# Smallest query tile of a sparse-attention stage: scores of two heads in one PSUM bank, maxima subtracted by VectorE, one exponential for four heads, and the units of the two small tiles alternated

## The chip, the cores and the metric

One core of one Trainium2 chip runs the kernel. The metric is the device time of one execution in microseconds (us); below, PE is TensorE, PEld its weight loads, DVE is VectorE, ACT is ScalarE, POOL is GpSimd and SP is the queue that issues most transfers.

## The reference, cut to what matters

A two-layer decoder trunk on 512 positions of width 1024. Layer 0 mixes with a gated linear recurrence and retention, layer 1 with sparse attention; each layer has a SwiGLU feed-forward part. The change lies in layer 1's attention. With 512 positions there are 8 blocks of 64, so the top 16 blocks are all blocks and the window of 512 covers everything: both the "selected" and the "window" branch are plain causal attention, each with its own keys and values.

```python
# 16 heads in 4 groups of 4; 64 elements a head; per branch: own k, v
s = jnp.einsum('bqgrd,bkgd->bgrqk', qb, kw)
p = jax.nn.softmax(jnp.where(causal, s, NEG), axis=-1)
o_branch = jnp.einsum('bgrqk,bkgd->bqgrd', p, vw)
o = gate0 * o_cmp + gate1 * o_slc + gate2 * o_win   # o_cmp: 31 compressed blocks
return o.reshape(B, QB, HD)                         # and then out @ w_out
```

## The kernel before, in words

All heavy products are done as three float32r products of a high and a low part (hi·hi, hi·lo, lo·hi). Before the attention stage the kernel runs layer 0 with its feed-forward part and layer 1's input projections; after it comes the output projection (`ps_p`, in `layer1`, with weights `w1o`), then the second feed-forward part.

`attention` cuts the 512 queries into four tiles of 128. Tile i sees (i+1)·128 keys. The order is tile 2, tile 3, tile 1, tile 0. The work is a list of units. For tiles 2 and 3 a unit is one group of 4 heads and one branch; for tiles 1 and 0 a unit is one group and both branches, so u.n is 2. That makes 8 + 8 + 4 + 4 = 24 units, numbered 0 to 23: units 16 to 19 are tile 1, units 20 to 23 are tile 0. The loop runs n from 0 to 26 in slots, at least four for each n. Three units are in work at once:

- unit n has its heads done, one head r in each slot. `head_s` (lines 1154 to 1167) puts the scores of one head for its branches in one PSUM bank (two products with the keys, hi and lo, and one product that adds the causal mask on the last 128 keys); `head_m` (L1171) takes the negated maximum on DVE; `head_e` (L1175) takes one exponential per branch on ACT, with the maximum as its bias; each is followed by a second instruction that reads out the row sum.
- unit n-1 is normalized: `norm` (L1179, L1180) takes reciprocals on DVE and multiplies them by the gates on POOL, `scale` (L1185) multiplies each head and branch on POOL.
- unit n-3 has its probability blocks of 128 keys turned and multiplied by the values, one block in each slot: `block_t` (L1190, four transposes on PE), `block_hi` (L1194, ACT), `block_lo` (L1197, DVE), `block_v` (L1205, L1206; at a group's end also L1211, L1212 for the compressed branch). `finish` (L1217 ACT, L1222 twice on DVE, L1226 ACT, L1228 POOL) then writes the group's output `o` as hi and lo parts, `oh` and `ol`.

Work of other kinds is given out a step at a time by `advance` from the list `side`: the steps of `finish`, the stacking of a tile's queries (`late`), and the compressed branch (`compressed`: scores on PE, mask and maximum on DVE, subtraction on POOL, exponential on ACT, sums on DVE, multiplication on POOL, transposes, hi and lo copies). The last product of a group (`br == 1 and j == u.i`) needs the tile's compressed probabilities:

```python
while u.i not in cmp_pt:
    advance()
```

The probabilities of a unit lie in a ring of four buffers (`probs`, tile `wr`), which is the ring that the weights are loaded to as well: the transfers of `w1o` wait for buffers of the last units. Scores have four PSUM banks (`psA`), transposes two (`psC`), outputs two (`psB`). A planner puts the instructions of each engine in order from the order of the program, shifted by the offsets of `high_priority`, and from its own estimates of when each is ready; on the chip every engine then runs its list strictly in that order.

Of the kernel before, what the change touches and what calls it, by code (L numbers as in the profile page):

```python
# [17 lines left out]
F32 = mybir.dt.float32  # L18
F32R = mybir.dt.float32r
AF = mybir.ActivationFunctionType  # L20
ALU = mybir.AluOpType
AX = mybir.AxisListType
PSUM = bass.MemoryType.PSUM

P = 128
# [8 lines left out]
G = 4  # L34
# [29 lines left out]
class Trunk:  # L64
# [1018 lines left out]
    def attention(self, QS, stack, stacked, qlate, halves, KH, KL, VV, kc2, vc, gate, OH, OL, fill):  # L1083
# [3 lines left out]
        V, A, Q, T = nc.vector, nc.scalar, nc.gpsimd, nc.tensor  # L1087
# [61 lines left out]
        def make(i, g, bs):  # L1149
            u = Unit()  # L1150
            u.i, u.g, u.bs, u.nk, u.n = i, g, bs, (i + 1) * P, len(bs)
            u.heads = [(u, r) for r in range(R)]
            u.blocks = [(u, b, j) for b in range(u.n) for j in range(i + 1)]
            return u

        def head_s(u, r):
            if r == 0:
                u.p = self.probs().rearrange("p (r b x) -> p r b x", r=R, b=u.n)
                u.rs = self.sm.tile([P, R, u.n], F32, tag="rs", name="rs")
                u.kh, u.kl = (x[u.g // 2][:, u.bs[0]:u.bs[-1] + 1, u.g % 2, 0:u.nk] for x in (KH, KL))  # L1160
            h = R * u.g + r
            ps = self.psA("ps_s")
            u.ps = ps[:, 0:u.n * u.nk].rearrange("p (b x) -> p b x", b=u.n)
            q = QS[u.i][:, h, :]
            T.matmul(u.ps, q, u.kh, start=True, stop=False)
            T.matmul(u.ps, q, u.kl, start=False, stop=False)
            T.matmul(u.ps[:, :, u.i * P:u.nk], self.identr, self.triNeg.unsqueeze(1).broadcast_to([P, u.n, P]), start=False, stop=True)

        def head_m(u, r):
            u.nm = self.sm.tile([P, 2], F32, tag="nm", name="nm")  # L1170
            V.tensor_reduce(u.nm[:, 0:u.n], u.ps, axis=AX.X, op=ALU.max, negate=True)  # L1171

        def head_e(u, r):
            for b in range(u.n):
                A.activation(u.p[:, r, b, 0:u.nk], u.ps[:, b, :], AF.Exp, bias=u.nm[:, b:b + 1], accum_out=u.rs[:, r, b:b + 1])  # L1175

        def norm(u):
            gb = gate[:, u.i, :].rearrange("p (h b) -> p h b", b=3)[:, R * u.g:R * u.g + R, u.bs[0] + 1:u.bs[-1] + 2]
            V.reciprocal(u.rs, u.rs)  # L1179
            Q.tensor_tensor(u.rs, u.rs, gb, op=ALU.mult)  # L1180

        def scale(u, r):
            for b in range(u.n):
                x = u.p[:, r, b, 0:u.nk]
                Q.tensor_tensor(x, x, u.rs[:, r, b:b + 1].broadcast_to([P, u.nk]), op=ALU.mult)  # L1185
# [43 lines left out]
            yield  # L1229

        tiles = halves[0] + halves[1]
        units = [make(i, g, bs) for i in tiles for g in range(G) for bs in (((0,), (1,)) if i >= 2 else ((0, 1),))]
        side = [compressed(tiles[0])]

        def advance():
# [7 lines left out]
        for n in range(len(units) + LAG):  # L1243
# [9 lines left out]
            for sl in range(max(R, nb)):  # L1253
# [5 lines left out]
                if hd:  # L1259
                    head_s(*hd)  # L1260
                if bl:
                    block_t(*bl)
                if hd:
                    with prio(offset=12):
                        head_m(*hd)
                if bl:
                    block_hi(*bl)
                if hd:
                    with prio(offset=-6):
                        head_e(*hd)  # L1270
# [3 lines left out]
                if un and sl < R:  # L1274
                    if sl == 0:
                        with prio(offset=-6):
                            norm(un)
                    scale(un, sl)
                if len(pend) >= 2:
                    args = pend.pop(0)  # L1280
                    block_v(*args)
                    u, b, j = args[:3]
# [145 lines left out]
```

## Time and profile before

| | |
|---|---|
| median of 3 runs | 1245.33 us (1245.04 to 1245.99) |
| the profiled execution, its own time | 1245.73 us |
| its span, first to last instruction | 1243.8 us |
| busy, whole span: PE, DVE, ACT, POOL | 98%, 64%, 55%, 19% |
| attention units 16 to 23, with what follows up to the gapless projection | 781.5 to 846.5 us |

The times of runs are made without the profiler's span: the profiled execution's own time is 1.9 us longer than its span, and 0.4 us longer than the median. Shares of busy time are averages over stages with different limits, so the stretch of the change is read by itself. [...]

### The profile page before, as it was taken

To read this page: it belongs to the slowest core of one execution; us is meant where nothing else is said; L and a number is where in the kernel's file an instruction comes from. 1 tells how busy PE (TensorE), PEld (TensorE's weight loads), DVE (VectorE), ACT (ScalarE), POOL (GpSimd) and SP (SyncE) were. 2 spreads that over 40 slices of the span, in tenths; PEclk is the share of its full clock that TensorE was granted. 3 is DMA by queue.
4 is the path that set the end of the run, shared out by engine and by line. 5 is a ranking of instruction groups with operands and counts; after the bars stand their busy time and mean duration, and the time that the engine had idled before them with its cause. 6 is when DMAs were issued, how large, how long until landed. Compare 5 with 4: busy or idle time off the path is not lost.

```text
span 1243.8 us, 16442 instructions
## 1 busy us (share of the span) xinstructions
PE 1221.5 (98%) x6077; PEld 1031.4 (83%) x6077; DVE 799.1 (64%) x1237; ACT 686.3 (55%) x1395; POOL 232.0 (19%) x303
## 2 busy tenths in 40 slices
PE   9999999999999999999999999999999999999997
PEld 7688888888888889988888878877888888888996
DVE  6886629666356636674364889986776537653764
ACT  6541447664256426655454688995666336633653
POOL 0001420220012002100000568680111011101200
PEclk9999999999999999999999999999999999999998
DMA  9122143784388328852100000134488358824832
GB/s 342 68 102 68 35 169 102 172 191 150 98 191 178 138 64 182 228 194 71 66 35 1 1 1 1 35 113 159 108 197 186 120 120 185 201 82 106 181 93 68
DMA packets 35535, 149.23 MB, mean 120 GB/s; under 512 B 3936, under 2 KB 6256, under 8 KB 26624
## 3 DMA queue, kind: packets, MB, share of 16 engines
q1 hardware_dynamic: 21296, 100.88, 22.8%
q0 software_dynamic: 14016, 47.27, 21.4%
q8 instruction: 48, 0.79, 0.2%
q14 instruction: 31, 0.25, 0.1%
q10 hardware_dynamic: 144, 0.04, 0.0%
HBM read 143.98 MB, written 4.19 MB: 119 GB/s over the span
## 4 chain that ended last, share of the span: by engine, by line
PE 88%; ACT 5%; DVE 4%; POOL 1%; issue 1%; DMA 0%; POOLq 0%; DVEq 0%; SPq 0%; ACTq 0%
PE ps L203 6%; PE ps L201 6%; PE ps L202 6%; PE ps_t L201 5%; PE ps_X L201 5%; PE ps_X L203 5%; PE ps_X L202 5%; PE ps_t L203 5%; PE ps_t L202 5%; PE ps_V L201 3%; PE ps_V L203 3%; PE ps_V L202 3%; ACT prob L1175 2%; PE ps_Y L201 2%; PE ps_Z L203 2%; PE ps_Z L201 2%
## 5 line engine op out<-in xcount | busy, mean ns | idle before, releaser
L136 ACT CAST whi<-wr 128x512 fp32r<-128x512 f32 (+1 forms) x540 | 295.1, 593 | 348.1 <-PE ps L202 126.2
L137 DVE TENSOR_TENSOR wlo<-wr,whi 128x1024 fp32r<-128x1024 f32 (+2 forms) x272 | 313.3, 1154 | 208.9 <-ACT whi L136 205.4
L201 PE MATMUL ps<-gh,whi 128*128 128x512 f32 (+1 forms) x364 | 139.8, 384 | 0.0
L203 PE MATMUL ps<-gh,wlo 128*128 128x512 f32 (+1 forms) x364 | 139.2, 382 | 0.0
L202 PE MATMUL ps<-gl,whi 128*128 128x512 f32 (+1 forms) x364 | 139.1, 382 | 0.0
L161 POOL DMA_DIRECT2D wr<-wff x64 | 55.6, 868 | 366.8 <-DVE wlo L137 327.8
L201 PE MATMUL ps_t<-whi,hgh 128*128 128x512 f32 x288 | 114.7, 399 | 0.0
L202 PE MATMUL ps_t<-wlo,hgh 128*128 128x512 f32 x288 | 113.3, 394 | 0.0
L203 PE MATMUL ps_t<-whi,hgl 128*128 128x512 f32 x288 | 112.7, 391 | 0.0
L201 PE MATMUL ps_X<-whi,sg 128*128 128x512 f32 (+1 forms) x288 | 107.2, 372 | 0.0
L203 PE MATMUL ps_X<-whi,sg 128*128 128x512 f32 (+1 forms) x288 | 106.9, 371 | 0.0
L202 PE MATMUL ps_X<-wlo,sg 128*128 128x512 f32 (+1 forms) x288 | 106.8, 371 | 0.0
L1185 POOL TENSOR_TENSOR prob<-prob,rs 128x384 f32<-128x384 f32 (+3 forms) x128 | 88.1, 722 | 1.9
L767 DVE TENSOR_TENSOR h<-ps,h 128x512 f32<-128x512 f32 x46 | 31.8, 691 | 82.6 <-PE ps L203 82.6
L203 PEld LDWEIGHTS ps<-gh,wlo 128*128 128x128 f32 x364 | 68.4, 188 | 13.3
L202 PEld LDWEIGHTS ps<-gl,whi 128*128 128x128 f32 x364 | 68.4, 188 | 13.2
L201 PEld LDWEIGHTS ps<-gh,whi 128*128 128x128 f32 x364 | 68.4, 188 | 13.0
L1175 ACT ACTIVATE prob<-ps_s,nm 128x384 f32<-128x384 f32 (+3 forms) x128 | 68.2, 540 | 15.8 <-DVE nm L1171 14.9
L201 PE MATMUL ps_V<-whi,sg 128*128 128x512 f32 (+1 forms) x192 | 71.2, 371 | 0.0
L202 PE MATMUL ps_V<-wlo,sg 128*128 128x512 f32 (+1 forms) x192 | 71.2, 371 | 0.0
L203 PE MATMUL ps_V<-whi,sg 128*128 128x512 f32 (+1 forms) x192 | 71.2, 371 | 0.0
L203 PEld LDWEIGHTS ps_t<-whi,hgl 128*128 128x128 f32 x288 | 54.1, 188 | 11.5 <-issue 0.2
(316 smaller groups left out, 2568.6 us busy)
## 6 DMA issues: line engine op xcount, KB each, us to landing
wr<-wff POOLq DMA_DIRECT2D x64, 512.0 KB, 5.9
wr<-wff SPq DMA_DIRECT2D x24, 1024.0 KB, 4.8
wr<-wfg POOLq DMA_DIRECT2D x32, 384.0 KB, 5.8
wr<-w0t SPq DMA_DIRECT2D x10, 1024.0 KB, 5.9
wr<-w1t SPq DMA_DIRECT2D x10, 1024.0 KB, 4.9
wr<-wfg SPq DMA_DIRECT2D x12, 768.0 KB, 4.3
wr<-w2a SPq DMA_DIRECT2D x8, 1024.0 KB, 4.8
wr<-w2c SPq DMA_DIRECT2D x8, 1024.0 KB, 5.0
```

Of the source, the lines that this page charges most:

```text
L136: self.nc.scalar.copy(hi[:, c], x[:, c])
L137: self.nc.vector.tensor_tensor(lo, x, hi.bitcast(F32), op=ALU.subtract)
L161: self.nc.gpsimd.dma_start(x[:, c], more[:, c], accum_op=ALU.add)
L201: mm(ps, ah, bh, start=(first and k == 0), stop=False)
L202: mm(ps, ah, bl, start=False, stop=False)
L203: mm(ps, al, bh, start=False, stop=(last and k == n - 1))
L767: V.tensor_tensor(hm, ps, hm, op=ALU.add)
L1175: A.activation(u.p[:, r, b, 0:u.nk], u.ps[:, b, :], AF.Exp, bias=u.nm[:, b:b + 1], accum_out=u.rs[:, r, b:b + 1])
L1185: Q.tensor_tensor(x, x, u.rs[:, r, b:b + 1].broadcast_to([P, u.nk]), op=ALU.mult)
```

## The change

For tile 0 alone (u.i == 0):

- `head_s` puts the scores of two heads, both branches, in one bank; the mask is added once for the pair, on 512 columns.
- `head_m` takes the maxima once for the pair (four maxima of 128 elements each, 512 in all), not negated.
- `head_e` subtracts the maxima on DVE, from PSUM into the probability buffer, once for each pair; after the fourth head ACT takes one exponential of the unit's 1024 elements in place, without bias and without row sums.
- `norm` takes the row sums on DVE, one reduction over 1024 elements.
- `scale` multiplies both branches of a head in one POOL instruction.

The list of units becomes tile 1, tile 0, tile 1, tile 0, and so on, a group at a time: units 16, 18, 20, 22 are tile 1 and units 17, 19, 21, 23 are tile 0.

```diff
         def head_s(u, r):
             ...
+            q = QS[u.i][:, h, :]
+            if u.i == 0:
+                if r % 2 == 0:
+                    u.ps = self.psA("ps_s").rearrange("p (r b x) -> p r b x", r=2, b=2)
+                T.matmul(u.ps[:, r % 2], q, u.kh, start=(r % 2 == 0), stop=False, skip_group_check=True)
+                T.matmul(u.ps[:, r % 2], q, u.kl, start=False, stop=False, skip_group_check=True)
+                if r % 2:
+                    T.matmul(u.ps.rearrange("p r b x -> p (r b) x"), self.identr, self.triNeg.unsqueeze(1).broadcast_to([P, 4, P]), start=False, stop=True, skip_group_check=True)
+                return
         ...
         def head_m(u, r):
-            u.nm = self.sm.tile([P, 2], F32, tag="nm", name="nm")
+            if u.i == 0 and r % 2 == 0:
+                return
+            u.nm = self.sm.tile([P, 4], F32, tag="nm", name="nm")
+            if u.i == 0:
+                V.tensor_reduce(u.nm, u.ps.rearrange("p r b x -> p (r b) x"), axis=AX.X, op=ALU.max)
+                return
             V.tensor_reduce(u.nm[:, 0:u.n], u.ps, axis=AX.X, op=ALU.max, negate=True)
         def head_e(u, r):
+            if u.i == 0:
+                if r % 2:
+                    x = u.p[:, r - 1:r + 1, :, 0:P].rearrange("p r b x -> p (r b) x")
+                    V.tensor_tensor(x, u.ps.rearrange("p r b x -> p (r b) x"), u.nm.unsqueeze(2).broadcast_to([P, 4, P]), op=ALU.subtract)
+                if r == 3:
+                    x = u.p[:, :, :, 0:P].rearrange("p r b x -> p (r b) x")
+                    A.activation(x, x, AF.Exp)
+                return
             ...
         def norm(u):
             ...
+            if u.i == 0:
+                V.tensor_reduce(u.rs.rearrange("p r b -> p (r b)"), u.p[:, :, :, 0:P].rearrange("p r b x -> p (r b) x"), axis=AX.X, op=ALU.add)
             V.reciprocal(u.rs, u.rs)
             ...
         def scale(u, r):
+            if u.i == 0:
+                x = u.p[:, r, :, 0:P]
+                Q.tensor_tensor(x, x, u.rs[:, r, :].unsqueeze(2).broadcast_to([P, 2, P]), op=ALU.mult)
+                return
             ...
-        units = [make(i, g, bs) for i in tiles for g in range(G) for bs in (((0,), (1,)) if i >= 2 else ((0, 1),))]
+        units = [make(i, g, bs) for i in halves[0] for g in range(G) for bs in ((0,), (1,))]
+        units += [make(i, g, (0, 1)) for g in range(G) for i in halves[1]]
```

## Rows read from the trace of the kernel before

**Rows 1.** The page, part 1: busy us, share of the span, instructions.
```profile
PE 1221.5 (98%) x6077; PEld 1031.4 (83%) x6077; DVE 799.1 (64%) x1237; ACT 686.3 (55%) x1395; POOL 232.0 (19%) x303
```
**Rows 2.** Stretches: us, then busy PE, PEld, DVE, ACT, POOL; PE clock; DMA share, GB/s.
```profile
740.00:800.00 60.00, 59.11 (x359) 48.89 (x358) 56.47 (x105) 54.17 (x142) 42.83 (x56) 1.00 0.06 19
781.50:806.00 24.50, 24.27 (x151) 20.42 (x149) 22.71 (x42) 23.30 (x76) 15.39 (x25) 1.00 0.14 44
806.00:836.00 30.00, 29.21 (x184) 23.96 (x183) 26.61 (x60) 29.52 (x108) 24.88 (x54) 1.00 0.23 77
836.00:846.50 10.50, 7.29 (x37) 5.43 (x36) 7.63 (x15) 9.39 (x20) 5.82 (x12) 1.00 0.76 283
...
846.50:852.00 5.50, 5.50 (x17) 4.41 (x18) 3.88 (x3) 0.00 (x0) 0.53 (x1) 0.69 0.53 167
```
**Rows 3.** Chain of work that ended last, 806 to 846.5 us, shares by line.
```profile
by line: ACT prob L1175 33.0%; ACT pth L1194 23.5%; ACT up L1217 9.4%; ACT whi L136 8.3%; issue 7.4%; ACT oh L1226 3.9%; DVE wlo L137 3.1%; POOL pcmp L1114 2.6%; DVE ptl L1197 1.7%; PE ps_tr L1190 1.6%; ACT pch L1135 1.6%; DVE mx L1112 1.5%
```
**Rows 4.** PE in order of time, 802.8 to 804.6 us: start, duration, engine, line.
```profile
802.86 0.40 PE L1166 MATMUL ps_s<-kl,qs 128*128 128x512 f32 x1
803.10 0.28 PE L1167 MATMUL ps_s<-triNeg,identr 128*128 128x256 f32 x1
803.22 0.60 PE L1190 MATMUL ps_tr<-ident,prob 128*128 128x128 f32 x4
...
804.57 0.28 PE L1167 MATMUL ps_s<-triNeg,identr 128*128 128x256 f32 x1
```
**Rows 5.** DVE in order of time, 811.0 to 812.1 us.
```profile
811.08 0.69 DVE L1197 TENSOR_TENSOR ptl<-ps_tr,pth 128x512 fp32r<-128x512 f32 x1
811.68 0.41 DVE L1171 TENSOR_REDUCE nm<-ps_s 128x2 f32<-128x256 f32 x1
812.02 0.19 DVE L1179 RECIPROCAL rs<-rs 128x8 f32<-128x8 f32 x1
```
**Rows 6.** DVE in order of time: the last unit's reciprocals.
```profile
835.15 0.20 DVE L1179 RECIPROCAL rs<-rs 128x8 f32<-128x8 f32 x1 [0.32 <-ACT prob L1175]
```
**Rows 7.** Groups by shape, 781.5 to 846.5 us: count | busy us, mean ns | idle before.
```profile
L1197 DVE TENSOR_TENSOR ptl<-ps_tr,pth 128x512 fp32r<-128x512 f32 x37 | 25.2, 681 | 4.0 <-ACT pth L1194 3.6
...
L1185 POOL TENSOR_TENSOR prob<-prob,rs 128x256 f32<-128x256 f32 x32 | 18.5, 614 | 0.3
...
L1175 ACT ACTIVATE prob<-ps_s,nm 128x128 f32<-128x128 f32 x32 | 12.3, 402 | 0.1
L1185 POOL TENSOR_TENSOR prob<-prob,rs 128x128 f32<-128x128 f32 x32 | 11.7, 400 | 0.3
L1171 DVE TENSOR_REDUCE nm<-ps_s 128x2 f32<-128x512 f32 x16 | 11.0, 686 | 0.4 <-PE ps_s L1167 0.2
...
L1171 DVE TENSOR_REDUCE nm<-ps_s 128x2 f32<-128x256 f32 x16 | 6.7, 418 | 0.2
```
**Rows 8.** Groups by shape, whole span: the nearest to the new instructions.
```profile
L865 DVE TENSOR_REDUCE pes<-pew 128x64 f32<-128x1024 f32 x2 | 4.0, 1983 | 0.0
...
L1175 ACT ACTIVATE prob<-ps_s,nm 128x512 f32<-128x512 f32 x32 | 22.1, 691 | 3.1 <-DVE nm L1171 2.7
```
**Rows 9.** ACT in order of time, 814.4 to 814.9 us.
```profile
814.47 0.37 ACT L1175 ACTIVATE prob<-ps_s,nm 128x128 f32<-128x128 f32 x1
...
814.83 0.36 ACT L1175 ACTIVATE prob<-ps_s,nm 128x128 f32<-128x128 f32 x1
```
**Rows 10.** All engines in order of time, 845.2 to 846.5 us.
```profile
845.21 2.90 DVE L137 TENSOR_TENSOR wlo<-wr,whi 128x1024 fp32r<-128x1024 f32 x2 [0.19 <-ACT whi L136]
...
846.49 0.50 PE L203 MATMUL ps_p<-oh,wlo 128*128 128x512 f32 x1 [2.64 <-DVE wlo L137]
```
**Rows 11.** SP's queue, 825 to 850 us: issues of the projection's weights.
```profile
831.53 9.27 SPq L117 DMA_DIRECT2D wr<-w1o  x4
```
**Rows 12.** Chain of waits, 660 to 880 us: tile 0's compressed branch.
```profile
806.25 1.06 POOL pcmp L1114
...
830.23 0.64 ACT pch L1135
```

More of the change, by code (lines that the diff above doesn't have):

```diff
@@ L1161, in head_s @@
             h = R * u.g + r
+            q = QS[u.i][:, h, :]
[7 more added lines that the diff above has]
+                return
             ps = self.psA("ps_s")
             u.ps = ps[:, 0:u.n * u.nk].rearrange("p (b x) -> p b x", b=u.n)
-            q = QS[u.i][:, h, :]
             T.matmul(u.ps, q, u.kh, start=True, stop=False)
```

## The prediction

> **What bounds the kernel now.** I read the page first: PE is busy over 98% of the span [rows 1], and that is an average. So I cut out the stretch of units 16 to 23, from 781.5 us to where the projection runs gaplessly at 846.5 us, and read it in three pieces [rows 2]. Up to 806 us PE is busy for 24.27 of 24.50 us. That could be modelled ends, so I looked at starts: from one mask product to the next is one slot, 804.57 - 803.10 = 1.47 us, and it is full of products [rows 4]. From 806 to 836 us ACT is busy for 29.52 of 30.00 us, and the chain of waits from 806 to 846.5 us runs over ACT: 33.0% exponentials, 23.5% casts of turned blocks [rows 3]. From 836 us everything thins out. [...]
>
> The reader is to see a third engine too. DVE is busy for 22.71 + 26.61 + 7.63 = 56.95 of these 65.0 us; it has 8.05 us free, 2.87 of them after 836 us [rows 2].
>
> **The change part by part.** Queues without gaps cost the distance of starts. On DVE a 512-element instruction lets the next start after 811.68 - 811.08 = 0.60 us, the 256-element maximum after 812.02 - 811.68 = 0.34 us [rows 5]; they last 681 to 686 and 418 ns [rows 7].
>
> DVE. Removed: 16 maxima of 256 elements, 16 x 0.34 = 5.4 us. Added: 8 maxima of 512, 8 x 0.60 = 4.8 us. Added: 8 subtractions of 512 elements out of PSUM; their nearest row is the 512-element subtraction of the low parts, also out of PSUM, so 8 x 0.60 = 4.8 us. Added: 4 sums over 1024 elements of SBUF. The trace has no such sum with neighbouring elements. From below, two 512-element reductions packed are 1.2 us; from above stands the strided reduction of 1024 elements at 1.98 us [rows 8]. The new one reads neighbours in runs of 128, like the maxima, so I take 1.2: 4.8 us, and keep 7.9 as the upper end. Net: 4.8 + 4.8 + 4.8 - 5.4 = +9.0 us, at most +12.1.
>
> [...]
>
> ACT. Removed: 32 exponentials of 128 with their read-outs, which start 814.83 - 814.47 = 0.36 us apart [rows 9], 11.5 us. Added: 4 of 1024 elements. Lasting 402 ns at 128 [rows 7] and 691 ns at 512 [rows 8], they grow by 0.075 us per 100 elements, so 1024 lasts 1.08 us: 4.3 us. Net -7.2 us. Its bounds are one and two of the 512-element kind, 0.69 and 1.38 us each, so net -8.7 to -6.0 us; with either, ACT has room.
>
> POOL. 32 multiplications of 128 become 16 of 256: 11.7 us become 16 x 0.614 = 9.8 us [rows 7], -1.9 us. POOL is busy for 46.1 of 65 us [rows 2]; nothing on the path.
>
> PE. 16 masks of 256 columns (803.22 - 803.10 = 0.12 us) become 8 of 512 (803.10 - 802.86 = 0.24 us) [rows 4]: 1.9 us either way, nothing. Eight weight loads less lie behind products.
>
> Order. Alternating mixes units with heavy heads (tile 1: PE 0.24 + 0.24 + 0.12 = 0.60 us a head) and light ones (tile 0: 3 x 0.12 = 0.36 us). The three last passes, which have no heads left, get 2 + 4 + 2 blocks in place of 2 + 2 + 2. Tile 0's queries are needed at unit 17 in place of unit 20; they are stacked in the first two slots of unit 16 as now, three slots ahead, so I cost this at nothing; without that cover PE waits for one cast and one subtraction, some 1.2 us. Groups 0 and 1 are finished for all tiles earlier than now, so more of the projection may run inside the tail.
>
> What the freed ACT time buys is limited by PE. Units 20 to 23 take (835.15 - 812.02) / 4 = 5.78 us each [rows 5, 6]. PE alone needs, without heads, 1.47 - 0.60 = 0.87 us a slot, with a head of tile 0 1.23 us, four slots 4.9 us, and two products for the compressed branch at 0.24: 5.4 us. So ACT's relief is worth at most 4 x 0.4 = 1.6 us, while DVE gets more work than it has time: 56.95 + 9.0 = 65.95 us in a stretch of 65.0.
>
> The sum. DVE can't be packed fully. Where it was the most pressed engine beside PE, it was busy for 56.47 of 60 us, 94% [rows 2]; with ACT relieved (3.6 of its 4.0 us idle before the low parts were waits for ACT's cast [rows 7]) I take 96% up to the tail, 2.2 us of 55, and 2.0 us idle in the tail (now 2.87). The stretch then takes 65.95 + 2.2 + 2.0 = 70.15 us, +5.2 us. Against that, PE has time free in the tail: now eight projection products (1.9 us) run ahead of its 2.64 us stop; I credit 2.0 us more, since groups 0 and 1 are ready earlier. Its bounds are 0 (the weights are issued from 831.53 us as buffers of units 20 to 23 come free [rows 11], and those now come free no sooner) and 2.64 + 1.7 = 4.3 us (no stop, no slow clock). So +5.2 - 2.0 = +3.2 us. The profiled execution becomes 1243.8 + 3.2 = 1247.0 us of span, 1.9 around it, 1248.9; against its median, 0.4 lower, 1248.5.
>
> **The rivals.**
>
> Stalled chain. The last product of tile 0's first group moves from n = 24 of the loop to n = 21. Counting the steps that the code hands out, one or two a slot, the compressed branch of tile 0 has by then come to its sums only (the subtraction and the exponential are given out two slots before); multiplication, transposes and copies are pressed out in one slot. Now this chain stretches from 806.25 to 830.23 us [rows 12]. Pressed together it is two POOL steps of 1.06, an exponential and a copy of 0.64 and two DVE steps of about 0.7 us each, 4.8 us, behind whatever stands in their queues; two slots (2.9 us) cover it in part. If PE stands there, 2 to 4 us come on top: 1251.5 us. Against it: the planner can put other units' blocks ahead. DVE's total doesn't depend on it.
>
> A wash. DVE's excess is taken up because the projection's products fill PE meanwhile: PE's work is unchanged, and whatever of it moves ahead of the end counts. At the credit's full 4.3 us: +0.9 us, 1246.2 us. The same comes out if tail idling on DVE vanishes.
>
> Faster. ACT is the chain from 806 us on; that chain loses 7.2 us, and mixing the units evens out PE's and ACT's stretches. Priced by the rows: 1.6 us in units 20 to 23 until PE bounds them, and 1.7 to 4.3 us in the tail, if the stop at 846.49 us and its slow clock go: -3.3 to -5.9 us, say 1241.0. The point from which it decides is DVE's packing: it needs the added 9.0 us of DVE to fit in 8.05 us free time, with gapless starts, or to end after PE no longer waits for it. That is the weak place. [...] The trace shows the changing engine (PE, then ACT), but also a third one, DVE, that is busy for 93% and 89% of the two pieces [rows 2].
>
> **How the numbers follow.** About 0.2% (2.5 us) is what a measurement of this kernel can tell from no change. Forecast (DVE becomes the bound, 1248.5): 0.42. Stalled chain (1251.5): 0.12. Wash: 0.29. Faster: 0.17. So slower 0.54, same 0.29, faster 0.17. The range reaches from 1242.0, which leaves about a tenth below (most of the faster case lies between it and 1241), to 1254.0: the forecast with DVE idling at 6% before the tail and no credit is +1.1 + 2.0 above 1248.5, the dear sums add 3.1, together 1254.7, and a stall alone stays below. The likeliest case's own range is 1247 to 1252.
>
> **What would show it.** In the profile after: on DVE 8 maxima, 8 subtractions and 4 sums for 16 maxima; a sum's duration near 1.3 us (right) or near 2 (dearer); the big exponential near 1.1 us; ACT's busy share in the stretch down by 7 us or so; DVE at 94% or more from 782 us to the tail, and the chain of waits there over DVE's low parts, subtractions and sums in place of exponentials. The stretch's end moved from 846.5 to about 850 us. Wrong: PE gapless through the stretch with DVE below 92% (then the packing was better than thought), the stop before the first low-part product gone, or PE waiting at L1211 for the compressed copies (stalled chain).

## The result, and the profile after

The kernel after the change takes 1253.96 us (median of 6 runs, 1252.56 to 1254.52); before, beside it, 1245.18 us (6 runs, 1244.67 to 1246.30). The ratio is 1.0067, with a 95% interval from 1.0055 to 1.0080: slower by about 8.3 us (the two medians differ by 8.8). The forecast was slower by 3.2 us, 1248.5 us, and its range ended at 1254.0. The direction was right, the size is more than double the forecast's, and the time lies 0.04 us inside the range's edge.

Part 1 of the page of the kernel after, its profiled execution (1254.29 us), answers to [rows 1]:

```profile
span 1252.5 us, 16337 instructions
...
PE 1226.2 (98%) x6069; PEld 1030.6 (82%) x6069; DVE 807.0 (64%) x1241; ACT 679.7 (54%) x1335; POOL 229.3 (18%) x287
```

The whole-span shares moved by a point at most; the change can't be judged there. DVE gained 7.9 us, ACT lost 6.6 and POOL 2.7, as the forecast has them within 1.1 us. The stretches of the kernel after, columns as in [rows 2]:

```profile
740.00:800.00 60.00, 59.16 (x364) 49.38 (x363) 56.75 (x106) 51.71 (x126) 42.73 (x54) 1.00 0.06 19
781.50:806.00 24.50, 24.14 (x151) 20.17 (x150) 23.43 (x43) 19.90 (x55) 13.03 (x21) 1.00 0.14 44
806.00:822.00 16.00, 13.89 (x78) 10.54 (x76) 15.33 (x30) 11.01 (x29) 12.13 (x22) 1.00 0.19 67
822.00:836.00 14.00, 9.91 (x49) 7.66 (x49) 9.32 (x17) 7.66 (x21) 5.50 (x10) 0.76 0.00 0
836.00:846.50 10.50, 9.26 (x50) 6.06 (x48) 9.54 (x19) 8.33 (x19) 8.37 (x17) 1.00 0.47 147
846.50:856.00 9.50, 9.14 (x42) 6.00 (x42) 6.46 (x11) 8.54 (x18) 2.98 (x5) 1.00 0.65 241
```

Until 800 us PE keeps its pace: 59.16 of 60.00 us, before 59.11. Then two things show. From 781.5 to 822 us DVE is busy for 23.43 of 24.50 and 15.33 of 16.00 us, 96% in both, and from 806 us on PE falls to 13.89 of 16.00 where it had 29.21 of 30.00. From 822 to 836 us every engine drops together, and PE's granted clock is 0.76. No engine is busy for more than 9.91 of these 14.00 us, so none bounds the stretch by its amount of work: something in it waits for one chain. Groups by shape of the kernel after from 781.5 to 856 us (answers to [rows 7]) first say what the new instructions cost:

```profile
L1210 POOL TENSOR_TENSOR prob<-prob,rs 128x256 f32<-128x256 f32 x16 | 9.3, 613 | 0.3
L1183 DVE TENSOR_REDUCE nm<-ps_s 128x4 f32<-128x512 f32 x8 | 5.5, 682 | 0.1
L1192 DVE TENSOR_TENSOR prob<-ps_s,nm 128x512 f32<-128x512 f32 x8 | 5.5, 681 | 0.0
L1203 DVE TENSOR_REDUCE rs<-prob 128x8 f32<-128x1024 f32 x4 | 4.8, 1211 | 0.0
L1195 ACT ACTIVATE prob<-prob 128x1024 f32<-128x1024 f32 x4 | 4.2, 1058 | 0.0
```

In durations, 5.5 + 5.5 + 4.8 less the 6.7 us of the old maxima is +9.1 us on DVE. The forecast's +9.0 is in distances of starts, though, which are shorter. DVE of the kernel after in order of time (as [rows 5]) gives these:

```profile
811.47 0.68 DVE L1192 TENSOR_TENSOR prob<-ps_s,nm 128x512 f32<-128x512 f32 x1
812.07 0.68 DVE L1226 TENSOR_TENSOR ptl<-ps_tr,pth 128x512 fp32r<-128x512 f32 x1
...
813.86 1.21 DVE L1203 TENSOR_REDUCE rs<-prob 128x8 f32<-128x1024 f32 x1
...
814.99 0.68 DVE L1226 TENSOR_TENSOR ptl<-ps_tr,pth 128x512 fp32r<-128x512 f32 x1
```

After a subtraction the next starts 0.60 us later, after a sum 1.13 us later. By these, the added work is 4.8 + 4.8 + 4 x 1.13 - 5.4 = +8.7 us. Next the chain of work of the kernel after, 806 to 822 us, in shares by line (as [rows 3]); the line breaks off in the view:

```profile
by line: DVE ptl L1226 15.6%; DVE nm L1185 15.3%; POOL prob L1214 14.6%; DVE rs L1203 7.0%; ACT pth L1223 6.7%; ACT prob L1198 6.4%; PE ps_tr L1219 4.9%; DVE o L1251 4.6%; DVE prob L1192 3.7%; ACT up L1246 3.6%; issue 3.3%; POOL ol L1257 2.
```

The five DVE lines shown add up to 46.2% where ACT's exponentials led before. The two longest are old work of DVE, the low parts (L1226) and tile 1's maxima (L1185); the new sums and subtractions are 10.7%. The hole after 822 us is found in order of time. POOL's instructions of the kernel after from 820 us:

```profile
819.82 4.61 POOL L1214 TENSOR_TENSOR prob<-prob,rs 128x256 f32<-128x256 f32 x8
824.39 1.05 POOL L1127 TENSOR_TENSOR pcmp<-pcmp,sc 128x512 f32<-128x512 f32 x1
```

and all engines of the same kernel in order of time (the bracket is the idle time before, and who ended it):

```profile
821.00 0.61 DVE L1125 TENSOR_SCALAR sc<-sc,tab 128x16 f32<-128x16 f32 x1
...
825.49 1.11 PE L1133 MATMUL ps_tr<-ident,pcmp 128*128 128x128 f32 x4 [3.44 <-POOL pcmp L1127]
...
826.64 0.59 ACT L1135 CAST pch<-ps_tr 128x512 fp32r<-128x512 f32 x1 [7.37 <-PE ps_tr L1133]
...
827.26 0.69 DVE L1136 TENSOR_TENSOR pcl<-ps_tr,pch 128x512 fp32r<-128x512 f32 x1 [3.86 <-ACT pch L1135]
```

Tile 0's compressed branch stands in a row: POOL's last multiplication of it (L1127) has its operand at 821.61 us (L1125) but is queued behind eight scalings of tile 1, 4.61 us in all, PE's transposes of its result (L1133) are already next in PE's list, and PE stands for 3.44 us, ACT for 7.37, DVE for 3.86. Before, the multiplication stood 8 us ahead of the transposes, here POOL and PE of the kernel before in order of time:

```profile
821.53 1.05 POOL L1127 TENSOR_TENSOR pcmp<-pcmp,sc 128x512 f32<-128x512 f32 x1
...
829.52 0.60 PE L1133 MATMUL ps_tr<-ident,pcmp 128*128 128x128 f32 x4
```

The end of the stretch in the kernel after, all engines in order of time (answers to [rows 10]), and the issues of the projection's weights on SP's queue (answers to [rows 11]):

```profile
854.42 1.21 DVE L137 TENSOR_TENSOR wlo<-wr,whi 128x1024 fp32r<-128x1024 f32 x1
...
855.13 0.40 PE L1241 MATMUL ps_o<-pcl,vc 128*128 128x512 f32 x1
...
855.69 0.50 PE L203 MATMUL ps_p<-oh,wlo 128*128 128x512 f32 x1 [0.16 <-DVE wlo L137]
```

```profile
840.35 12.84 SPq L117 DMA_DIRECT2D wr<-w1o  x4
```

The counterpart of the last attention product in the kernel before, PE in order of time:

```profile
843.00 0.39 PE L1212 MATMUL ps_o<-pcl,vc 128*128 128x512 f32 x1
```

The two traces don't run level even where nothing was changed. Here is an instruction from the start of attention, long before the changed units, ACT in order of time, in the kernel before and in the kernel after:

```profile
674.44 1.18 ACT L1027 CAST qs<-ps_tr 64x512 fp32r<-64x512 f32 x2 [0.33 <-DVE qs L1028]
```

```profile
674.79 1.18 ACT L1027 CAST qs<-ps_tr 64x512 fp32r<-64x512 f32 x2 [0.33 <-DVE qs L1028]
```

So 0.35 us has to come off each difference of times. The last attention product starts 12.1 us later, 11.8 without that lag; the weights are issued 8.8 us later, 8.5 without it. The hand-over from the last attention product to the first low part of the projection shrinks from 3.49 to 0.56 us. So 2.9 us come back and 8.9 of the 11.8 stay. The tail's slow clock of [rows 2] is gone (1.00 from 855 to 862 us), and one came up at 822 us instead.

### The profile page after: what moved, and what is told of

Its sections match the earlier page's. It is cut to its first block, busy times and chain, and to the rows that moved or that the text cites. A ratio compares the mean times of both kernels' runs of the same rounds, so it can differ in the third digit from the quotient of the medians.

```text
span 1252.5 us, 16337 instructions
## 1 busy us (share of the span) xinstructions
PE 1226.2 (98%) x6069; PEld 1030.6 (82%) x6069; DVE 807.0 (64%) x1241; ACT 679.7 (54%) x1335; POOL 229.3 (18%) x287
## 4 chain that ended last, share of the span: by engine, by line
PE 83%; DVE 5%; ACT 5%; DMA 2%; POOL 2%; issue 2%; POOLq 0%; DVEq 0%; SPq 0%; ACTq 0%
PE ps L201 6%; PE ps L203 6%; PE ps L202 6%; PE ps_t L201 5%; PE ps_t L203 5%; PE ps_t L202 5%; PE ps_X L201 4%; PE ps_X L203 4%; PE ps_X L202 4%; PE ps_V L201 3%; PE ps_V L203 3%; PE ps_V L202 3%; DMA wr<-wfg 2%; PE ps_Z L201 2%; PE ps_Z L203 2%
## 5 line engine op out<-in xcount | busy, mean ns | idle before, releaser
L1214 POOL TENSOR_TENSOR prob<-prob,rs 128x384 f32<-128x384 f32 (+2 forms) x96 | 76.4, 828 | 1.6
L1198 ACT ACTIVATE prob<-ps_s,nm 128x384 f32<-128x384 f32 (+2 forms) x96 | 55.9, 587 | 16.1 <-DVE nm L1185 15.3
```

## The experiments

The theories: **O** (the new order presses tile 0's compressed branch, and PE stands behind it), **D** (DVE gets more work than it has room for), and against D **L** (not DVE's amount of work, but that a head's path from scores to probabilities became longer). The recorded expectations below use letters of their own and explain them where they stand. On the chips used, runs of the kernel before spread from 1244.3 to 1250.7 us, so only ratios to the runs beside each kernel are compared; 0.0010 is 1.25 us.

**1 and 2: each half of the change alone.** e1 has the new heads with the old order, e2 the old heads with the new order.

```diff
 e1, against the kernel after
-        units = [make(i, g, bs) for i in halves[0] for g in range(G) for bs in ((0,), (1,))]
-        units += [make(i, g, (0, 1)) for g in range(G) for i in halves[1]]
+        units = [make(i, g, bs) for i in tiles for g in range(G) for bs in (((0,), (1,)) if i >= 2 else ((0, 1),))]
 e2, against the kernel before: the same lines the other way round
```

> The changed heads of tile 0 alone; units in the old order (all of tile 1, then all of tile 0), so tile 0's compressed branch keeps its old place and its chain isn't pressed. Theory A (two costs: DVE's 9 us more work costs 4 to 6 us, the pressed chain with PE's stop and its slow clock 3 to 5 us): 1249 to 1251 us. Rival D (DVE's total alone sets the end, the stop only shows where DVE is late): the whole loss, 1253 to 1255 us. Rival S (the stop alone, DVE's work is absorbed): 1244.5 to 1246.5 us.

> The alternated order alone, with the old heads: DVE's work stays as before, ACT keeps its 32 small exponentials, the compressed branch of tile 0 is pressed as in the changed kernel. Theory A: 1248 to 1250 us, with PE standing at the compressed branch's transposes for 2 us or more. Rival D: as before or faster, 1243 to 1246 us. Rival S: the whole loss, 1252 to 1255 us.

Measured: heads 1.0035 (1.0025 to 1.0044), order 1.0035 (1.0021 to 1.0048). The product is 1.0070 against 1.0067 for both together: the halves add up, and each is worth some 4.4 us. In e2 PE stops at the same line as after, but for 1.50 us, less than the 2 us expected, here in order of time:

```profile
821.66 0.66 PE L1133 MATMUL ps_tr<-ident,pcmp 128*128 128x128 f32 x4 [1.50 <-POOL pcmp L1127]
```

In e1 there is no such stop.

**3 and 4: the compressed branch handed out sooner.** Two steps a slot from n = 16 to 20, in the kernel after (e3) and in e2 (e4).

```diff
-                for _ in range(2 if len(side) > 2 else 1):
+                for _ in range(2 if len(side) > 2 or 16 <= n <= 20 else 1):
```

> The changed kernel with two side steps a slot in n = 16 to 20, so that the compressed branch of tile 0 is given out by n = 18 and not pressed at n = 21. DVE's work stays as in the changed kernel. Theory A: 1249 to 1251 us, no stop of PE at the compressed transposes, no slow clock there, DVE at 94% or more up to the tail. Rival D: 1253 to 1255 us (the end hangs on DVE's total). Rival S: 1244.5 to 1246.5 us.

> Old heads, alternated order, compressed branch given out early: neither DVE's added work nor the pressed chain. All theories: about the time of before. Theory A and S: 1243 to 1246 us. Rival D: 1243 to 1246 us. If it is above 1247 us, the alternated order costs by itself (its longer last passes, the later weights of the projection), and all three are incomplete.

Measured: 1.0055 (1.0037 to 1.0072) and 1.0029 (1.0020 to 1.0038); both missed. The stop didn't go, it moved: 2.2 us in e3 by its waits, and in e4, in order of time:

```profile
805.01 0.66 PE L1133 MATMUL ps_tr<-ident,pcmp 128*128 128x128 f32 x4 [2.13 <-POOL pcmp L1127]
```

The earlier start alone didn't help: only one idle step still lay between POOL's multiplication and PE's transposes. So the next runs widen that distance.

**5, 6 and 11: the distance.** The earlier start of 3 and 4, and seven idle steps in place of one: e5 is after with both, e6 has old heads with the new order and both, e11 is before with both.

```diff
-            yield
+            for _ in range(7 if i == 0 else 1):
+                yield
             pt = self.psC("ps_tr")
```

> The changed kernel with two side steps a slot in n = 16 to 20, and seven idle steps in place of one between the multiplication of tile 0's compressed branch and its transposes, so that PE no longer comes to them before POOL is done. Theory P (the alternated order costs because PE stands at those transposes; heads and order add up): only the heads' cost is left, ratio 1.003 to 1.0045, no stop at the transposes. Rival T (the order costs in the tail: longer last passes, the projection's weights issued 4 us later): ratio stays at 1.0055 to 1.007.

> The same spacing with the old heads and the alternated order. Theory P: ratio 0.999 to 1.001, no stop at the compressed transposes. Rival T: ratio 1.0025 to 1.0035, as with the order alone.

> Control: the kernel before, old heads and old order, with the two side steps a slot and the seven idle steps. The old order doesn't press the chain, so nothing should be won by spacing it: 0.999 to 1.001. If it is at 0.999 or lower like the spaced alternated order, that order's small gain belongs to the spacing and not to the alternation.

Measured: e5 1.0033 (1.0023 to 1.0042), e6 0.9991 (0.9982 to 1.0000), e11 1.0022 (1.0011 to 1.0033). The stop at L1133 is gone in e5 and e6, and with it 3.4 and 4.4 thousandths, 4.2 and 5.5 us. With the branch spaced the alternation costs nothing, so the rival that it costs in the tail (T in the expectations) falls. The last attention product is at 845.84 us in e6, at 850.04 in e2. The named stop is only 1.50 us of that 4.20, though; the edit also lays out the lists anew, and stop and layout can't be told apart by it. e11 missed: in the old order the same edit costs 2.7 us, so it is no improvement for its own sake, and what it recovers in the new order isn't its own gift. The heads' price is seen again between e5 and e6: 4.2 thousandths, 5.2 us, in the new order, beside 4.4 us in the old one (part of the 5.2 is a stop that is told under 9 and 12). Here is the stretch from 806 to 836 us of e1, e5 and e6, in that order, columns as in [rows 2]:

```profile
806.00:836.00 30.00, 27.33 (x163) 21.35 (x162) 29.25 (x56) 20.71 (x43) 19.89 (x36) 1.00 0.15 40
```

```profile
806.00:836.00 30.00, 27.59 (x158) 21.33 (x156) 28.46 (x53) 23.84 (x67) 20.39 (x38) 1.00 0.11 36
```

```profile
806.00:836.00 30.00, 28.19 (x167) 22.61 (x165) 24.93 (x50) 29.23 (x106) 24.05 (x52) 1.00 0.20 70
```

With the new heads DVE is busy for 29.25 and 28.46 of 30 us and ACT has 6 to 9 us to spare; with the old ones ACT is full and DVE has 5 us free. No slow clock shows in any.

**7 and 8: D against L.** e7 is e1 without the row sum: it leaves out a normalization by the right sum, and takes an estimated 1 us a unit both off DVE and out of the path (by distances of starts 1.13 us for the sum of the kernel after, in place of 0.11 as from before's reciprocals of eight elements at 806.09 us to the next start at 806.20), so it can't tell D from L by itself. e8 is before with 15 unread maxima on DVE.

```diff
 e7, against e1
-                V.tensor_reduce(u.rs..., u.p[:, :, :, 0:P]..., axis=AX.X, op=ALU.add)
+                V.tensor_scalar(u.rs, u.p[:, :, :, 0], 1.0, None, op0=ALU.add)
 e8, against before, ahead of a head's maximum
+            if u.i == 0 and (u.g, r) != (3, 3):
+                V.tensor_reduce(nx, self.tab[:, 0:512]..., axis=AX.X, op=ALU.max)
```

> The changed heads in the old order, with the row sums left out: in place of the sum over 1024 elements DVE adds one to the first element of each of the eight rows, so the instruction waits for the exponential as before but lasts some 0.1 us; the output is not normalized rightly. DVE has 4.4 us less to do. Theory D (the heads cost by DVE's busy time): of the heads' 1.0035 some 1.000 to 1.0015 is left. Rival L (they cost by the longer path from scores over maximum, subtraction, exponential and sum to the probabilities): 1.0025 to 1.0035.

> The kernel before with 15 further DVE reductions of 512 elements of a constant table, one at each head of tile 0 but the last; nothing reads their results. DVE gets 15 x 0.60 = 9.0 us more, nothing else changes, no path gets longer. Theory D: ratio 1.0025 to 1.005 (ACT isn't relieved here). Rival L: 0.999 to 1.001.

Measured: e7 1.0009 (1.0000 to 1.0018), e8 1.0043 (1.0030 to 1.0056). e8 shows that more DVE time is enough: 15 x 0.60 = 9.0 us by distance of starts, whose results nobody reads, cost 5.4 us, about as much as the heads, with ACT's work unchanged. Its group by shape, and its stretch from 806 to 836 us:

```profile
L1171 DVE TENSOR_REDUCE nx<-tab 128x4 f32<-128x512 f32 x15 | 10.2, 678 | 0.1
```

```profile
806.00:836.00 30.00, 26.83 (x162) 21.77 (x162) 29.42 (x65) 25.73 (x91) 20.79 (x42) 1.00 0.10 36
```

DVE is full (29.42 of 30.00) and PE falls to 26.83, much as in e1 (29.25 and 27.33). But the expectation that no path gets longer isn't met, as DVE of e8 shows in order of time:

```profile
811.50 0.69 DVE L1171 TENSOR_REDUCE nx<-tab 128x4 f32<-128x512 f32 x1
812.10 0.41 DVE L1173 TENSOR_REDUCE nm<-ps_s 128x2 f32<-128x256 f32 x1
```

The unread maximum stands right ahead of the head's own one, so a head's path is 0.60 us longer here too, and e8 can't exclude L either. What speaks for D is the idle time: a path that is too long would let DVE stand and wait, but DVE stands for only 0.75 us of the 30 in e1 and 0.58 in e8, and before for 3.39. That D is the main cause in this stretch is thus argued from full queues, not shown by a run that leaves the path alone.

**10: bank pairing alone.** e5 with 32 exponentials as before, each with its bias and row sum on ACT; two heads still share a bank, a maximum and a mask, and POOL scales both branches at once. No subtraction and no sum on DVE.

```diff
-                V.tensor_reduce(u.nm, u.ps..., axis=AX.X, op=ALU.max)
+                V.tensor_reduce(u.nm, u.ps..., axis=AX.X, op=ALU.max, negate=True)
...
-                    V.tensor_tensor(x, u.ps..., u.nm..., op=ALU.subtract)
-                if r == 3:
-                    A.activation(x, x, AF.Exp)
+                    for z in range(2):
+                        for b in range(2):
+                            A.activation(u.p[:, r - 1 + z, b, 0:P], u.ps[:, z, b, :], AF.Exp, bias=..., accum_out=...)
...
-                V.tensor_reduce(u.rs..., u.p..., axis=AX.X, op=ALU.add)
```

> The spaced chain and the alternated order, with only the cheap part of the new heads: two heads' scores in a bank, one maximum for the pair (8 x 0.60 in place of 16 x 0.34 us on DVE, 0.6 us less), one mask for the pair, one POOL multiplication for both branches; ACT keeps its 32 exponentials with bias and row sums. If the loss lay in the subtractions and sums alone, about the spaced order without new heads: 0.998 to 1.0005. If sharing a bank costs by itself (two heads' scores wait for one another), above 1.001.

Measured: 1.0019 (1.0006 to 1.0033), between e6 (0.9991, at most 1.0000) and e5 (1.0033, at least 1.0023). The pairing keeps some cost of its own against e6, which DVE's time doesn't explain, as DVE has 0.6 us less to do; that stays open. That taking subtraction and sum off DVE recovers a part against e5 is likely, but the intervals overlap.

**9 and 12: half the heads.** New heads in groups 0 and 2 only: e9 on e5, e12 on e1. The edit puts the condition into every branch of the heads:

```diff
+            u.new = i == 0 and g % 2 == 0
-            if u.i == 0:
+            if u.new:
```

> The spaced chain and the alternated order, with the new heads in two of tile 0's four units only (groups 0 and 2), so DVE gets 4.5 us more and ACT 3.6 us less. Without new heads this order stood at ratio 0.9991, with all four at 1.0033. If DVE's cost sets in only once its free time is used up, 0.999 to 1.0005; if every microsecond on DVE costs its share, 1.001 to 1.002.

> The old order of units and no spacing, with the new heads in two of tile 0's four units (groups 0 and 2): DVE 4.5 us more, ACT 3.6 us less, the compressed branch where it was. All four units so cost ratio 1.0035. If DVE absorbs what fits in its free time: 0.999 to 1.0008. If every microsecond on DVE costs its share: 1.0014 to 1.0022. Above 1.003, as with half the heads in the spaced order, the cost doesn't follow the amount of DVE work at all, and the theory of DVE's busy time falls.

Measured: e9 1.0041 (1.0026 to 1.0057), e12 1.0031 (1.0021 to 1.0040). Both missed: half of DVE's added work costs as much time as all of it. By its recorded expectation, e12 above 1.003 is where the theory of DVE's busy time falls; its interval reaches below that mark.

The traces of the old order show how far the theory carries. The cast L1027 that stands at 674.44 us before starts at 674.71 us in e1, 675.29 in e8, 676.00 in e7 and 676.08 in e12; with these lags taken off, the last attention product lies behind the one before by 0.8 us in e12 and 1.7 in e7, with about 4.5 us added on DVE, and by 6.5 us in e8 and 9.5 in e1, with about 9. So up to the end of attention the loss does grow with DVE's amount: much of the first 4.5 us is taken up, little of the second. (2, 6, 6 and 13 products of the projection, in that order, stand ahead of that last product, before 6; one is 0.23 us of PE by distance of starts.) In e12 most of the time is lost behind it, at the hand-over, in order of time:

```profile
845.47 0.39 PE L1242 MATMUL ps_o<-pcl,vc 128*128 128x512 f32 x1
...
850.82 0.50 PE L203 MATMUL ps_p<-oh,wlo 128*128 128x512 f32 x1 [3.58 <-DVE wlo L137]
```

From the last attention product to the first low part pass 5.35 us, before 3.49. Only 2 products of the projection were put ahead of the former, so PE stands for 3.58 us for the weights' low part. This low part comes 2.7 us later than before, the lag taken off; the rest of e12's 3.9 us isn't located. In e9 a part of the loss lies earlier:

```profile
793.00 0.20 POOL L1207 TENSOR_TENSOR rs<-rs,gate 128x8 f32<-128x8 f32 x1 [3.68 <-DVE rs L1206]
...
793.29 4.61 POOL L1216 TENSOR_TENSOR prob<-prob,rs 128x256 f32<-128x256 f32 x8
...
797.86 1.05 POOL L1114 TENSOR_TENSOR pcmp<-pcmp,mx 128x512 f32<-128x512 f32 x1
...
798.94 0.63 ACT L1116 ACTIVATE pcmp<-pcmp 128x512 f32<-128x512 f32 x1 [3.16 <-POOL pcmp L1114]
...
800.84 0.50 PE L1236 MATMUL ps_o<-pth,vv 128*128 128x512 f32 x1 [1.70 <-ACT pth L1225]
```

POOL runs eight scalings, the compressed branch's subtraction comes behind them, ACT stands for that, and PE for ACT's cast behind it. e5 and e3 have the same stop of 1.7 us, e10 one of 0.96, e6 none. POOL's run alone isn't the cause, for e6 has it too, its ACT in order of time with POOL's subtraction:

```profile
795.91 0.37 ACT L1176 ACTIVATE prob<-ps_s,nm 128x128 f32<-128x128 f32 x1
...
796.51 1.06 POOL L1114 TENSOR_TENSOR pcmp<-pcmp,mx 128x512 f32<-128x512 f32 x1
...
797.86 0.66 ACT L1116 ACTIVATE pcmp<-pcmp 128x512 f32<-128x512 f32 x1
```

With the old heads ACT fills that time with tile 0's small exponentials (L1176) and casts and comes to the compressed branch when it is ready. With the new ones it has none of these to do there, its exponential of the compressed branch is next in its list, and it stands for 3.16 us. So where the compressed branch is handed out early, the new heads have a second price, apart from DVE's amount, and it is part of the 5.2 us between e5 and e6. It isn't the merged exponential alone: e10, which keeps the small ones, has a shorter stop too.

## Why the prediction was right in direction and short in size

**The instruction prices held.** Net DVE was +9.0 us forecast and is +8.7 by distances of starts; the sum that was taken at 1.2 us has 1.13 (814.99 - 813.86; it lasts 1.211); the large exponential was put at 1.08 and lasts 1.058; POOL's scalings at 9.8 us took 9.3. The strided row of 1.98 us was rightly put aside.

**DVE became the bound, as forecast.** Its packing of 96% up to the tail came out at 96% in both stretches before the stop, its lines lead the chain, and e8 shows that DVE load costs time. But the sign "94% or more to the tail" failed: from 822 to 836 us DVE was busy for 9.32 of 14.00 us, since it too waited for the compressed branch. Of the signs of being wrong one came in full: the stop before the first low part is all but gone (0.16 us, before 2.64). The stretch ended at 855.7 us, not at about 850. The heads' term was +5.2 - 2.0 = +3.2 us; the heads alone measured 1.0035, 4.4 us. That these lie so close is luck, for both parts were too small and offset each other. In e1's trace the last attention product is 9.5 us later (1.6 of it for the seven products more of the projection ahead of it), so of the 8.05 us that DVE had free some 0.8 were usable for the new work (8.7 - 9.5 + 1.6), where the sum took 3.8. The tail gave back 5.0 (of 9.7 us at that product 4.7 are left in the span, 1248.5 against 1243.8 us). The credit's upper end was 4.3. Its 1.7 us of slow clock, (1 - 0.69) x 5.5 from [rows 2], shows in before's starts of products: 13 distances from 846.49 to 851.17 us take 4.68 us, and at the later pace of 0.23 us each they would take 3.0.

**The step that failed is "Order ... I cost this at nothing".** The order alone measured 1.0035, 4.4 us. The step looked at the queries of tile 0, which were indeed no matter. What the runs showed in its place is the stalled chain, which the prediction held as a rival at a chance of 0.12 and 2 to 4 us. PE's stop in that chain is shown (3.44 us after, 1.50 in e2), and it goes when the branch is spaced. The price was a little too low: 4.2 and 5.5 us between the kernels with and without the stop, the new layout of the lists included, and how much of these is the stop itself isn't shown. The chance was too low, and the place was one step off: PE stands not where the copies are used (L1211 of before), but one link sooner, at the transposes behind POOL's multiplication. The argument against it, that the planner can put other units' blocks ahead, didn't hold for those transposes: PE reached them 3.44 us before POOL was done. Forecast and rival weren't alternatives; both happened, and 1248.5 + 2 to 4 us is 1250.5 to 1252.5, still short by the rest of both terms. That 1253.96 us falls inside a range that ends at 1254.0 is luck: its upper end was added up from other terms than the ones that came true.

**The faster rival** needed DVE's work to fit in its free time. It didn't. Interleaving the units of the two small tiles, whose stretches PE and then ACT filled, was tried without the new heads in e6: 0.9991 (0.9982 to 1.0000). At best that is a gain of 0.2%, only with the compressed branch spaced, and without it the interleaving costs 1.0035. **The wash** failed with the order.

**What isn't settled.** The time doesn't follow DVE's amount, though the end of attention in the old order does: about 4.5 us more in e12 cost as much time as 9 in e1. e12 and e9 show where time went (the hand-over to the projection, ACT's wait for the compressed branch), not what made the planner put the lists so. D isn't cut off from L by a run that leaves a head's path alone. e10's rest and e11's 2.7 us have no shown cause. No kernel here clearly beats the one before; e6 is within what can be told from it.

## What to carry to other kernels

Before work is moved from the engine that the chain shows to another, read that other engine's busy share in the same stretch: 9 us on a DVE that was busy for 89% of the stretch cost 4 to 5.5 us, whether ACT gained or not. Take differences of times between two traces only after comparing an instruction ahead of the change: here two lay 1.6 us apart where nothing had changed yet. When units are reordered in queues that run in order (here a product whose low part DVE had done at 822.20 us started only at 827.11, behind the transposes that PE stood for), count for every side chain the steps between a producer on a bunched engine (here POOL, eight scalings in 4.61 us) and the consumer in PE's list, and price forecast and rival as a sum where both can happen. A half-sized version of an edit need not have half its cost when a planner lays out the rest anew (here e12's half cost 3.9 us, e1's whole 4.4).

## What the runs showed of the hardware that was not expected

PE's granted clock was 0.76 from 822 to 836 us of the kernel after: 0.52 from 822 to 825.49 us, in which PE stood for 3.44 us, 0.50 from there to 829 us, with PE busy all the time, and 1.00 from 829 to 836 us. That is (1 - 0.76) x 14 = 3.4 us of full-speed time, some 1.7 of it while PE stood anyway. The kernel e2, with a stop of 1.50 us at the same line, kept 1.00 from 822 to 836 us, and so did e1, in which PE was busy for 11.42 of these 14 us without a stop at that line. PE's four transposes right behind the stop took 1.11 us there and 0.66 us in e2. In this trace a slow clock thus came with a stop in the middle of a stretch. In e1 one came without a single long stop: the clock was 0.72 from 846.5 to 852 us, after a stretch of 10.5 us in which PE was busy for 7.12 us without a stop longer than 0.92.
